# An encoder layer on one core: the norm's weights applied per chunk of 512 tokens, and dummy transposes on TensorE

## The chip, the cores and the metric

The kernel runs on one core of a Trainium2 chip. The metric is the device time of one execution in microseconds; less is better. Before the change it is 1535.71 us, the median of three runs (1535.27 to 1535.77).

## What is computed

One layer of an encoder on 1024 tokens and 16 meta tokens, with 1024 features, in float32:

```python
h = jnp.concatenate([meta_tokens, x], axis=1)          # 16 + 1024 rows
a = rms_norm(h, norm_mix[l])                           # y = x * rsqrt(mean(x*x) + EPS) * g
(q_na, k_na, v_na, q_hg, z_f, z_b, i_hg, g_hg, gate_na, gate_hg) = split_cols(a @ w_in[l])
...
k_f, lf_f = gates(z_fwd, lb[0])                        # lb: a softmax over two rows of logits
k_b, lf_b = gates(z_bwd, lb[1])
...
h = h + mix @ w_o[l]
m = rms_norm(h, norm_mlp[l])
h = h + jnp.square(jax.nn.relu(m @ w_up[l])) @ w_down[l]
h = rms_norm(h, norm_final)
return h[:, N_META:]
```

The change touches only the first lines of this: the norm of the input, its transposition, and the first two products with `w_in`, for the gates `z_f` and `z_b` of the first of four recurrent heads.

## The kernel before

The tokens are cut into two halves (h = 0, 1) of 512. The normed input is held transposed, features on partitions, in `aT[h]`: two tiles of [128, 8, 512], a high part rounded to float32r (`aT_87` and `aT_89` in the lists below) and a low part, the remainder (`aT_88`, `aT_90`). The 16 meta tokens are columns 512 to 527 of half 0. The weights of a column block are split in the same way into `hi` and `lo`, and a product takes three matmuls for each of the eight chunks k of 128 features (`mm3`: L122 hi by high, L123 hi by low, L124 lo by high).

`start()` works on nine tiles of rows: x0 to x7 of 128 tokens and the meta rows `xm`. Each goes through four steps: ScalarE squares it and sums (L554); GpSimd makes the reciprocal root (L92, L93); VectorE multiplies the rows by it and by the norm's weights, which had been spread over all partitions by two products with a row of ones (L542, L545), in one instruction (L559); TensorE transposes eight blocks into two PSUM banks (L567), which ScalarE and VectorE evict as high and low part (L575, L576). Between the tiles stand steps of the first products: `first_products(d, h, ...)` makes gate direction d (0 forward, `z_f`; 1 backward, `z_b`) for a half. `start()` runs the first 256 tokens of direction 0 and half 0 of direction 1; `rest()` runs the others, the last of them direction 1, half 1. Then the projections of `hgrn` follow.

In this stretch the order on each engine is the order in which the code is written (`manual_schedule`). An engine works off its list strictly in order and waits on semaphores. PSUM has eight banks, handed out by tag: "mm" has two, "mx" two, "a" four, each tag in rotation. A new tile in a bank waits until the last reader of the tile that held it before is done, wherever that reader stands in the code:

```python
    banks = {"mm": ctx.enter_context(tc.tile_pool(name="ps_mm", bufs=2, space=PSUM))}
    psum_pools(mx=2, a=4)
```

After the products of one piece, `gates_of` evicts it with two sigmoids on ScalarE (L220, L221) and three instructions on VectorE (L222, L225). The loads of x and of the weight blocks are issued by SP, the small ones by ScalarE's queue.

Of the kernel before, what the change touches and what calls it, by code (L numbers as in the profile page):

```python
# [13 lines left out]
ALU = mybir.AluOpType  # L14
# [34 lines left out]
def layer(ctx: ExitStack, tc: tile.TileContext, x, meta, w_in, w_na, w_hg, w_o, w_up, w_dn,  # L49
# [154 lines left out]
    def gates_of(hd, hp, tiles, done=()):  # L204
# [30 lines left out]
        if hd == 0:  # L235
            yield
            for n_ in range(5):
                d, ps, t0, n, nm = done[n_]
                ev, mev = gate(d)
                if nm:  # L240
                    mev(ps[:, n:])
                ev(ps[:, :n], t0, n)
                yield
            return
# [255 lines left out]
    def first_products(d, h, c0, n, t0, nm):  # L500

        ps = mm_tile(n + nm)
        firsts.append((d, ps, t0, n, nm))
        hi, lo = blocks[d]
        for k in range(KC):
            mm3(ps, hi[:, k], lo[:, k], *(q[:, k, c0:c0 + n + nm] for q in aT[h]), k == 0, k == KC - 1)
            yield

    def start():
        p0s = ExitStack()  # L510
        p0 = p0s.enter_context(tc.tile_pool(name="p0", bufs=1, side="right", reuse_waits="tile"))
        g_bc = p0.tile([P, D], F32, name="g_bc")
        xm = p0.tile([NM, D], F32, name="xm")
        xt = [p0.tile([P, D], F32, tag="xt", name="xt", bufs=8) for _ in range(8)] + [xm]
        lt = p0.tile([P, 2, 2, NHG], F32, name="lt")
        mx = p0.tile([P, 2, NHG], F32, name="mx")
        g_row = p0.tile([1, D], F32, name="g_row")
        ones = p0.tile([1, P], F32, name="ones")
        na, rs = {}, {}
# [4 lines left out]
        def raw_of(col):  # L524
            return load_raw(w_in[:, col:col + P], KC)
        pool.memset(ones, 1.0)
        act.dma_start(g_row, g_mix.rearrange("(o d) -> o d", o=1))
        act.dma_start(xm, meta)
        act.dma_start(lt.rearrange("p a b c -> p (a b c)"), lbl)
        act.dma_start(gain_sb, gain)  # L530
        load_x(0)
        load_x(1)
        raw_f = raw_of(C_ZF)
        for i in range(2, 5):
            load_x(i)
        raw_b = raw_of(C_ZB)
        for i in range(5, 8):
            load_x(i)

        pgs = [bank("a", "pg").rearrange("p a b -> p (a b)") for h in range(2)]  # L540
        for h in range(2):
            pe.matmul(pgs[h], ones, g_row[:, h * TH:(h + 1) * TH], start=True, stop=True)  # L542

        def spread(h):
            act.copy(g_bc[:, h * TH:(h + 1) * TH], pgs[h])  # L545

        def rows(i):
            return NM if i == 8 else P

        def square(i):  # L550
            n = rows(i)
            ssq, rs[i], tm = (p0.tile([P, 1], F32, tag=t, name=t, bufs=6) for t in ("ssq", "rs", "rtm"))
            na[i] = p0.tile([P, D], F32, tag="na", name="na", bufs=4)
            act.activation(na[i][:n], xt[i][:n], AF.Square, accum_out=ssq[:n])  # L554
            rsqrt_mean(rs[i][:n], ssq[:n], D, tm[:n])

        def scale(i):
            n = rows(i)
            dve.scalar_tensor_tensor(na[i][:n], xt[i][:n], rs[i][:n], g_bc[:n], op0=ALU.mult, op1=ALU.mult)  # L559

        def transpose(i):
            n = rows(i)
            pts = []
            for j in range(2):
                pts.append(bank("a", "pt"))
                for k in range(4):
                    pe.transpose(pts[j][:, k, :n], na[i][:n, (4 * j + k) * P:(4 * j + k + 1) * P], ident[:n, :n])  # L567
            return pts

        def evict(i, pts):  # L570
            n = rows(i)
            c0, t = (TH, aT[0]) if i == 8 else (i % 4 * P, aT[i // 4])
            for j in range(2):
                hi, lo = (q[:, 4 * j:4 * j + 4, c0:c0 + n] for q in t)
                act.copy(hi, pts[j][:, :, :n])  # L575
                dve.tensor_tensor(lo, pts[j][:, :, :n], hi.bitcast(F32), op=ALU.subtract)  # L576
# [5 lines left out]
        pts = {}  # L582

        def turn(i):
            pts[i] = transpose(i)

        spread(0)
        square(0)
        spread(1)
        square(1)  # L590
        scale(0)
        turn(0)
        square(2)
        scale(1)
        evict(0, pts[0])
        turn(1)
        blocks[0] = load_block(None, KC, raw=raw_f)
        square(3)
        scale(2)
        evict(1, pts[1])  # L600
        turn(2)
        square(4)
        scale(3)
        evict(2, pts[2])
        f0 = first_products(0, 0, 0, 256, 0, 0)
        some(f0, 4)
        turn(3)
        square(5)
        scale(4)
        evict(3, pts[3])  # L610
        some(f0, 4)
        turn(4)
        square(6)
        blocks[1] = load_block(None, KC, raw=raw_b)
        scale(5)
        evict(4, pts[4])
        b0 = first_products(1, 0, 0, TH, 0, 0)
        some(b0, 2)
        turn(5)
        square(7)  # L620
        scale(6)
        evict(5, pts[5])
        some(b0, 2)
        turn(6)
        square(8)
        scale(7)
        evict(6, pts[6])
        some(b0, 2)
        turn(7)
        scale(8)  # L630
        dve.tensor_tensor(mx, lt[:, :, 0], lt[:, :, 1], op=ALU.max)
# [13 lines left out]
    def rest(gates):  # L645
# [3 lines left out]
        for d, q in ((0, (0, 1, 0, TH, TH, 0)), (0, (0, 0, 256, 256, 256, NM)), (1, (1, 1, 0, TH, TH, 0))):  # L649
            if d:  # L650
                early[C_Q] = block_of(C_Q)
# [975 lines left out]
```

## Time and profile before

| what | value |
|---|---|
| three timed runs | 1535.27 to 1535.77 us, median 1535.71 |
| the profiled execution, span from first to last instruction | 1534.6 us |
| TensorE busy | 1503.2 us, 98% of the span |
| VectorE, ScalarE, GpSimd busy | 67%, 43%, 25% |
| mean busy share of the DMA engines in the first 18 us | near 100% from 3 us on |

The profiled execution is another one than the timed ones, and its own time is known as its span. A busy share is an average over all stages. What a stage costs is read from the order of events in it: which instruction waited, and whose end released it.

### The profile page before, as it was taken

The numbers are of one execution on the slowest core, as the hardware profiler recorded it, in microseconds if no ns is written. First come the engines' busy times: TensorE is split into PE (matmuls) and PEld (weight loads), VectorE is DVE, ScalarE is ACT, GpSimd is POOL, SyncE is SP. The second block draws the span as 40 slices with busy tenths as digits, with TensorE's granted clock in tenths as the row PEclk, the third lists the DMA queues.
The fourth block names the chain that finished last, engine by engine and source line by source line (L and its number), as shares of the span: only waits on it lengthen the run. The fifth ranks groups of instructions, "written<-read, shape, count | busy, mean of one in ns | idle before, by whom it ended". The sixth has DMA issues, their size and how long they took to land.

```text
span 1534.6 us, 23451 instructions
## 1 busy us (share of the span) xinstructions
PE 1503.2 (98%) x9192; PEld 1252.2 (82%) x9192; DVE 1031.3 (67%) x1603; ACT 658.9 (43%) x1175; POOL 380.1 (25%) x354
## 2 busy tenths in 40 slices
PE   7999999999999998999999999999999999999998
PEld 5888888878888887888888887888888888888886
DVE  6676666654876877666476358877777544877876
ACT  6231313125665666434123135555555533434444
POOL 2323131316315400011000122533333300231142
PEclk9999999999999999999999999999999999999999
DMA  4111111114123128434746123444444676563224
GB/s 167 45 29 56 29 56 29 56 29 130 56 66 120 62 65 272 138 124 153 261 163 233 42 97 117 165 154 153 153 153 150 208 266 236 193 232 111 96 83 151
DMA packets 142449, 195.61 MB, mean 127 GB/s; under 512 B 8049, under 2 KB 90097, under 8 KB 142338
## 3 DMA queue, kind: packets, MB, share of 16 engines
q1 hardware_dynamic: 133216, 172.53, 33.9%
q10 hardware_dynamic: 6946, 14.24, 2.4%
q0 software_dynamic: 2176, 7.34, 1.3%
q8 instruction: 72, 1.18, 0.3%
q14 instruction: 39, 0.32, 0.1%
HBM read 139.56 MB, written 54.53 MB: 126 GB/s over the span
## 4 chain that ended last, share of the span: by engine, by line
PE 89%; DVE 5%; issue 2%; ACT 2%; DMA 1%; POOL 1%; ACTq 0%; POOLq 0%; SPq 0%; DVEq 0%
PE mm L122 11%; PE mm L123 11%; PE mm L124 11%; PE mm L1349 5%; PE pa L1349 4%; PE pb L856 4%; PE pb L858 4%; PE pb L857 4%; PE pc L1349 4%; PE pb L1349 4%; PE pc L858 3%; PE pc L857 3%; PE pc L856 3%; PE pa L858 2%; PE pa L857 2%
## 5 line engine op out<-in xcount | busy, mean ns | idle before, releaser
L122 PE MATMUL mm<-aT,hi 128*128 128x512 f32 (+2 forms) x640 | 229.8, 359 | 2.4 <-DVE QX L727 1.5
L124 PE MATMUL mm<-aT,lo 128*128 128x512 f32 (+2 forms) x640 | 226.9, 354 | 0.5 <-DVE lo L113 0.5
L123 PE MATMUL mm<-aT,hi 128*128 128x512 f32 (+2 forms) x640 | 225.8, 353 | 0.0
L122 PEld LDWEIGHTS mm<-aT,hi 128*128 128x128 f32 x640 | 121.4, 190 | 16.6 <-issue 1.7
L124 PEld LDWEIGHTS mm<-aT,lo 128*128 128x128 f32 x640 | 121.3, 190 | 14.2 <-DVE lo L113 1.0
L123 PEld LDWEIGHTS mm<-aT,hi 128*128 128x128 f32 x640 | 121.4, 190 | 12.5
L97 DVE TENSOR_TENSOR dl<-ur,dh 128x1024 fp32r<-128x1024 f32 x54 | 71.0, 1315 | 87.3 <-ACT dh L96 87.1
L96 ACT CAST dh<-ur 128x1024 fp32r<-128x1024 f32 x54 | 56.9, 1054 | 166.5 <-issue 91.1
L112 ACT CAST hi<-raw 128x1024 fp32r<-128x1024 f32 x36 | 37.8, 1050 | 96.7 <-PE mm L123 68.4
L1154 DVE TENSOR_TENSOR wl<-raw,wh 128x512 fp32r<-128x512 f32 x50 | 40.9, 822 | 36.5 <-ACT wh L1153 36.3
L1158 ACT ACTIVATE uv<-uv 128x512 f32<-128x512 f32 x48 | 30.4, 633 | 80.0 <-DVE uv L1266 48.9
L1154 DVE TENSOR_TENSOR wl<-sx,wh 128x512 fp32r<-128x512 f32 x70 | 61.0, 882 | 3.4 <-ACT wh L1153 3.3
L1153 ACT CAST wh<-sx 128x512 fp32r<-128x512 f32 x70 | 42.3, 620 | 42.3 <-PE pc L857 24.0
L1439 POOL TENSOR_TENSOR w<-w,tt 128x512 f32<-128x512 f32 x16 | 23.4, 1460 | 132.9 <-DVE tt L1438 113.2
L300 POOL TENSOR_TENSOR Y<-X,TN 128x512 f32<-128x512 f32 x20 | 34.3, 1713 | 84.5 <-DVE X L297 84.5
L113 DVE TENSOR_TENSOR lo<-raw,hi 128x1024 fp32r<-128x1024 f32 x36 | 46.8, 1300 | 9.8 <-ACT hi L112 9.7
L782 DVE CUSTOM_DVE_ANT_0 pr<-nsc,NB 128x432 f32<-128x432 f32 (+1 forms) x64 | 35.2, 560 | 26.7 <-PE nsc L777 26.5
L409 DVE TENSOR_TENSOR QQ<-QQ,TN 128x512 f32<-128x512 f32 x48 | 35.1, 742 | 22.9 <-PE sc L404 22.9
L856 PE MATMUL pb<-nt,wh 128*128 128x512 f32 x128 | 50.2, 392 | 0.3 <-DVE uv L1236 0.2
L122 PE MATMUL mm<-wh,mT 128*128 128x512 f32 x128 | 50.1, 392 | 0.0
L858 PE MATMUL pb<-nt,wl 128*128 128x512 f32 x128 | 49.8, 389 | 0.0
L124 PE MATMUL mm<-wh,mT 128*128 128x512 f32 x128 | 49.8, 389 | 0.0
(391 smaller groups left out, 4370.9 us busy)
## 6 DMA issues: line engine op xcount, KB each, us to landing
raw<-in_w_in SPq DMA_DIRECT2D x56, 512.0 KB, 4.0
ur<-usp SPq DMA_DIRECT2D x54, 512.0 KB, 3.4
raw<-in_w_up SPq DMA_DIRECT2D x16, 1024.0 KB, 6.1
usp<-us SPq DMA_DIRECT2D x60, 256.0 KB, 2.2
sg<-gsp SPq DMA_DIRECT2D x16, 512.0 KB, 3.3
w<-in_w_dn SPq DMA_DIRECT2D x16, 512.0 KB, 4.5
usp<-uv SPq DMA_DIRECT2D x30, 256.0 KB, 3.2
gsp<-gv ACTq DMA_DIRECT2D x24, 256.0 KB, 2.4
```

What stands on the lines that cost most here:

```text
L96: act.copy(hi, src)
L97: dve.tensor_tensor(lo, src, hi.bitcast(F32), op=ALU.subtract)
L113: dve.tensor_tensor(lo[:, :kc], raw[:, :kc], hi[:, :kc].bitcast(F32), op=ALU.subtract)
L122: pe.matmul(ps, lh, rh, start=first, stop=False)
L123: pe.matmul(ps, lh, rl, start=False, stop=False)
L124: pe.matmul(ps, ll, rh, start=False, stop=last)
L856: pe.matmul(ps, lhs[0][:, c], rhs[0][:, k], start=first and k == 0, stop=False, skip_group_check=True)
L857: pe.matmul(ps, lhs[0][:, c], rhs[1][:, k], start=False, stop=False, skip_group_check=True)
L858: pe.matmul(ps, lhs[1][:, c], rhs[0][:, k], start=False, stop=k == 3, skip_group_check=True)
L1153: act.copy(v(hi), src)
L1154: dve.tensor_tensor(v(lo), src, v(hi).bitcast(F32), op=ALU.subtract)
L1349: pe.matmul(ps, a[n == 2][:, q, j * P:(j + 1) * P], b[n == 1][:, q], start=first and n == 0, stop=last and n == 2, skip_group_check=True)
```

## The change

In the lists and in the code after the change, `warm` is a PSUM tile that nothing reads, `ptm` holds the transposed meta rows, `am` their product with the weights, f0, b0, f1 are the pieces of `first_products` (0, 0), (1, 0) and (0, 1).

- The rows are scaled by their reciprocal root alone, in place (`scale`). The weights come as a column `g_col` of [128, 8] (the host hands in the array in that shape) and are applied at the eviction, to 512 tokens of one chunk of features at a time (`evict(h, k)`): ScalarE writes the high part as a product with the column, VectorE the low part in one instruction. The spreading products and copies are gone.
- A bank now holds one chunk of features of four row tiles (`pts[h, k]`). In the first half six banks are filled side by side, chunks 6 and 7 follow between the first product steps.
- The meta rows come first; they are scaled and transposed into `ptm` in the second bank of tag "mm", and evicted late, behind the scaling of the second half.
- The split of the first two weight blocks is shared out: high part of block 0 on ScalarE, of block 1 on GpSimd, low parts in halves of 512 columns, one of four on VectorE and three on GpSimd.
- The row tile x7 is squared on VectorE. The softmax of `lbl` moves behind the first half's evictions. Half 0 is taken in one product of 512 columns, the 16 meta columns as a piece of their own. The first gate is evicted within `start()`.
- `keep_warm(n)` issues n transposes of the identity into `warm`: 26, then 10, 6, 6 and 5 between the real ones.
- The order of loads becomes x0 to x3, both weight blocks, x4 to x7.

```diff
-    def first_products(d, h, c0, n, t0, nm):
-        ps = mm_tile(n + nm)
-        firsts.append((d, ps, t0, n, nm))
+    def first_products(d, h, tag, n=TH):
+        nm = NM if n == NM else 0
+        c0 = TH if nm else 0
+        ps = bank(tag, "mm").rearrange("p a b -> p (a b)")[:, :n]
+        firsts.append((d, ps, h * TH, n - nm, nm))
...
         def scale(i):
-            n = rows(i)
-            dve.scalar_tensor_tensor(na[i][:n], xt[i][:n], rs[i][:n], g_bc[:n], op0=ALU.mult, op1=ALU.mult)
+            n = xt[i].shape[0]
+            tm = p0.tile([P, 1], F32, tag="rtm", name="rtm", bufs=9)
+            rsqrt_mean(rs[i][:n], sums[i][:n], D, tm[:n])
+            dve.tensor_scalar(xt[i], xt[i], rs[i][:n], None, op0=ALU.mult)
...
+        warm = bank("mm", "warm")
+        def keep_warm(n):
+            for j in range(n):
+                pe.transpose(warm[:, j % 4], ident, ident)
+        def turn(i, ks):
+            for k in ks:
+                pe.transpose(pts[i // 4, k][:, i % 4], xt[i][:, k * P:(k + 1) * P], ident)
+        def chunk(h, k):
+            pts[h, k] = bank("a", "pt")
+            for i in range(4 * h, 4 * h + 4):
+                turn(i, (k,))
+        def evict(h, k):
+            hi, lo = (t[:, k, :TH] for t in aT[h])
+            pt = pts[h, k].rearrange("p a b -> p (a b)")
+            act.mul(hi, pt, g_col[:, k:k + 1])
+            dve.scalar_tensor_tensor(lo, pt, g_col[:, k:k + 1], hi.bitcast(F32), op0=ALU.mult, op1=ALU.subtract)
...
+        keep_warm(26)
+        square(8)
+        scale(8)
+        ptm = bank("mm", "ptm")[:, 0].rearrange("p (k t) -> p k t", t=NM)
+        for k in range(KC):
+            pe.transpose(ptm[:, k], xt[8][:, k * P:(k + 1) * P], ident[:NM, :NM])
+        keep_warm(10)
+        for k in range(6):
+            pts[0, k] = bank("a" if k < 4 else "mx", "pt")
+        for i in range(4):
+            square(i)
+            scale(i)
+            turn(i, range(6))
+            if i < 3:
+                keep_warm(6 - i // 2)
+        block(0)
+        block(1)
+        low(0, dve, A)
+        low(0, pool, B)
+        low(1, pool, A)
+        low(1, pool, B)
+        f0 = first_products(0, 0, "mm")
+        evict(0, 0)
+        evict(0, 1)
+        for k in range(6):
+            some(f0, 1)
+            if k < 2:
+                chunk(0, k + 6)
+            evict(0, k + 2)
...
+        some(f0, 2)
+        for i in (4, 5, 6):
+            square(i)
+            if i == 4:
+                act.activation(lts, lts, AF.Exp)
+                pool.tensor_tensor(mx, lt[:, :, 0], lt[:, :, 1], op=ALU.add)
         scale(4)
+        square(7, dve)
+        for i in (5, 6, 7):
+            scale(i)
         dve.reciprocal(mx, mx)
...
+        b0 = first_products(1, 0, "mm")
+        some(b0, 6)
+        dve.tensor_tensor(am, ptm, fap(g_col, 0, [[1, KC], [0, NM]]), op=ALU.mult)
+        act.copy(mh, am)
+        dve.tensor_tensor(ml, am, mh.bitcast(F32), op=ALU.subtract)
+        f1 = first_products(0, 1, "mx")
+        for k in range(KC):
+            chunk(1, k)
+            evict(1, k)
+            if k == 0:
+                next(gates)
+            if k < 2:
+                some(b0, 1)
+            if k > 2:
+                some(f1, 1)
```

What stands on an engine's list shows where the change puts things. First the start of TensorE's list, before the change (`na` are the scaled rows, `pg` the spread weights; in brackets the engines whose semaphores the row waits for, Activation is ScalarE, Pool is GpSimd):

```order
L542 MATMUL pg<-g_row,ones 128x512 [waits DMAHW0_49,Pool_49]
L542 MATMUL pg<-g_row,ones 128x512
L567 MATMUL pt<-ident,na 128x128 [waits DVE_49]
L567 MATMUL pt<-ident,na 128x128 x7
L567 MATMUL pt<-ident,na 128x128 [waits DVE_49]
```

And after it:

```order
L557 MATMUL warm<-ident 128x128 [waits Pool_49]
L557 MATMUL warm<-ident 128x128 x25
L594 MATMUL ptm<-ident,xm 128x16 [waits DVE_49]
L594 MATMUL ptm<-ident,xm 128x16 x7
L557 MATMUL warm<-ident 128x128 x10
L561 MATMUL pt<-ident,xt 128x128 [waits DVE_49]
L561 MATMUL pt<-ident,xt 128x128 x5
L557 MATMUL warm<-ident 128x128 x6
```

The two spreading products are gone; 26 dummies, the meta transposes and ten more dummies stand ahead of the first rows of x, and six more behind them.

Next TensorE's list after the change where f0 ends and b0 begins (the last row of step 6 of f0, steps 7 and 8 cut short, and the first rows of b0):

```order
L124 MATMUL mm<-aT_87,lo 128x512
L122 MATMUL mm<-aT_87,hi 128x512 [waits Activation_49]
L123 MATMUL mm<-aT_88,hi 128x512 [waits DVE_49]
...
L124 MATMUL mm<-aT_87,lo 128x512
L122 MATMUL mm<-aT_87,hi 128x512 [waits DVE_49]
L123 MATMUL mm<-aT_88,hi 128x512
L124 MATMUL mm<-aT_87,lo 128x512 [waits Pool_49]
L122 MATMUL mm<-aT_87,hi 128x512
```

In f0 a first product (L122) waits for ScalarE, which wrote its operand `aT_87`. The first product of b0 reads the same `aT_87` and a `hi` that GpSimd wrote, and waits for VectorE.

Last VectorE's list after the change, from the end of the first half's evictions to the first of the second half:

```order
L572 SCALAR_TENSOR_TENSOR aT_88<-pt,g_col,aT_87 128x512 [waits Activation_49] x2
L551 TENSOR_SCALAR xt<-xt,rs 128x1024 [waits DMAHW2_49,Activation_49,Pool_49]
L544 ISA junk,ssq<-xt 128x1024 [waits DMAHW5_49,Activation_49]
L544 ISA ssq 128x1
L551 TENSOR_SCALAR xt<-xt,rs 128x1024 [waits DMAHW3_49,Pool_49]
L551 TENSOR_SCALAR xt<-xt,rs 128x1024 [waits DMAHW4_49,Activation_49,Pool_49]
L551 TENSOR_SCALAR xt<-xt,rs 128x1024 [waits DVE_49,Pool_49]
L632 RECIPROCAL mx<-mx 128x8
L637 TENSOR_TENSOR am<-ptm,g_col 128x128
L639 TENSOR_TENSOR aT_88<-am,aT_87 128x8x16 [waits Activation_49]
L572 SCALAR_TENSOR_TENSOR aT_90<-pt,g_col,aT_89 128x512 [waits Activation_49]
```

The only reader of `ptm` stands behind all four scalings of the second half. From the first product of the query block (`C_Q`) on, the lists of all engines hold the same computing work in the same order in both kernels.

## Rows read from the trace of the kernel before

**Rows 1.** The page: the span, and the chain that ended last by engine.

```profile
span 1534.6 us, 23451 instructions
...
PE 89%; DVE 5%; issue 2%; ACT 2%; DMA 1%; POOL 1%; ACTq 0%; POOLq 0%; SPq 0%; DVEq 0%
```

**Rows 2.** TensorE's waits, whole span: us in total, times, longest us.

```profile
PE pt L567 <- DVE na L559: 4.4, 2, 2.3
...
PE ppt L797 <- DVE PT L809: 2.6, 1, 2.6
```

**Rows 3.** Timeline of TensorE, 3 to 49 us: start, us, what, count.

```profile
3.31 3.75 PE L542 MATMUL pg<-g_row,ones 1*128 1x512 f32 x4 [3.31 <-DMA g_row<-in_g_mix]
9.33 3.97 PE L567 MATMUL pt<-ident,na 128*128 128x128 f32 x16 [2.27 <-DVE na L559]
15.46 1.94 PE L567 MATMUL pt<-ident,na 128*128 128x128 f32 x8 [2.17 <-DVE na L559]
...
19.76 1.91 PE L567 MATMUL pt<-ident,na 128*128 128x128 f32 x8
...
22.95 1.04 PE L567 MATMUL pt<-ident,na 128*128 128x128 f32 x8
...
29.27 1.07 PE L567 MATMUL pt<-ident,na 128*128 128x128 f32 x8
...
31.66 1.06 PE L567 MATMUL pt<-ident,na 128*128 128x128 f32 x8
...
48.25 0.39 PE L123 MATMUL mm<-aT,hi 128*128 128x512 f32 x1
48.47 0.39 PE L124 MATMUL mm<-aT,lo 128*128 128x512 f32 x1
```

**Rows 4.** Timeline, all engines, first 100 us: two of the issues of loads.

```profile
1.28 0.35 ACTq L528 DMA_DIRECT2D xm<-in_meta  x1
...
2.10 3.07 SPq L522 DMA_DIRECT2D xt<-in_x  x3
```

**Rows 5.** DMA view, issues at 1.28 and 2.10 us: KB each, us to landing.

```profile
xm<-in_meta ACTq DMA_DIRECT2D x1, 64.0 KB, 4.7
...
xt<-in_x SPq DMA_DIRECT2D x1, 512.0 KB, 7.2
```

**Rows 6.** Timeline of ScalarE: a square, two evictions, a table load.

```profile
5.87 1.06 ACT L554 ACTIVATE na<-xt 128x1024 f32<-128x1024 f32 x1
...
27.54 1.07 ACT L575 CAST aT<-pt 128x512 fp32r<-128x512 f32 x2 [1.24 <-PE pt L567]
...
34.99 1.28 ACT L220 ACT_TABLE_LOAD   x1
```

**Rows 7.** Timeline of VectorE: a scaling, two evictions, a tensor_scalar of 512 columns.

```profile
7.99 1.28 DVE L559 SCALAR_TENSOR_TENSOR na<-xt,rs,g_bc 128x1024 f32<-128x1024 f32 x1 [7.99 <-POOL rs L93]
...
15.23 1.28 DVE L576 TENSOR_TENSOR aT<-pt,aT 128x512 fp32r<-128x512 f32 x2
...
37.50 0.55 DVE L222 TENSOR_SCALAR T<-sf,oml_sb,lb_sb 128x512 f32<-128x512 f32 x1
```

**Rows 8.** Groups by form on GpSimd, whole span: busy us, mean ns, idle before.

```profile
L187 POOL TENSOR_TENSOR rt<-aT,aT 128x512 f32<-128x512 f32 x16 | 22.5, 1405 | 12.7 <-DMA tsp_t<-rt 12.2
...
L699 POOL MEMSET KL<- 64x1152 f32 x1 | 1.1, 1057 | 0.1
```

**Rows 9.** Stretches: length, busy of PE, PEld, DVE, ACT, POOL, clock, DMA, GB/s.

```profile
18.00:21.00 3.00, 3.00 (x16) 3.00 (x15) 2.10 (x3) 1.22 (x4) 1.54 (x2) 1.00 0.01 2
```

**Rows 10.** Timeline of TensorE in the attention stage: products of 128 columns.

```profile
395.50 0.22 PE L820 MATMUL pov<-PT,Vn 128*128 128x128 f32 x1
395.55 0.22 PE L821 MATMUL pov<-PT,Vn 128*64 128x128 f32 x1
```

**Rows 11.** Timeline of TensorE, its last product.

```profile
1527.16 0.39 PE L1349 MATMUL pa<-dh,dl 128*128 128x512 f32 x1
```

**Rows 12.** Stretches, the last one (columns as in rows 9).

```profile
1530.00:1534.60 4.60, 0.00 (x0) 0.00 (x0) 0.75 (x1) 0.72 (x1) 0.00 (x0) 0.53 0.59 228
```

More of the change, by code (lines that the diff above doesn't have):

```diff
@@ L538, in start @@
+        for i in range(4, 8):
             load_x(i)
[L540 to L550, printed above, removed]
-            n = rows(i)
[L552 to L555, printed above, removed]
@@ L557, in scale, with square @@
-        def scale(i):
-            n = rows(i)
-            dve.scalar_tensor_tensor(na[i][:n], xt[i][:n], rs[i][:n], g_bc[:n], op0=ALU.mult, op1=ALU.mult)
[L561 to L576, printed above, removed]
+        def square(i, eng=act):
+            t = xt[i]
+            n = t.shape[0]
+            sums[i], rs[i] = (p0.tile([P, 1], F32, tag=q, name=q, bufs=9) for q in ("ssq", "rs"))
+            junk = p0.tile([P, D], F32, tag="junk", name="junk", bufs=2)
+            if eng is act:
+                act.activation(junk[:n], t, AF.Square, accum_out=sums[i][:n])
+            else:
+                dve.tensor_tensor_reduce(out=junk[:n], in0=t, in1=t, scale=1.0, scalar=0.0,
+                                         op0=ALU.mult, op1=ALU.add, accum_out=sums[i][:n])
@@ L580, in some @@
                 next(steps)
[L582 to L605, printed above, removed]
@@ L628, in start, with block @@
[L628 to L631, printed above, removed]
-        pool.tensor_tensor(lt[:, :, 0], lt[:, :, 0], mx, op=ALU.subtract)
-        pool.tensor_tensor(lt[:, :, 1], lt[:, :, 1], mx, op=ALU.subtract)
-        some(b0, 2)
-        evict(7, pts[7])
-        turn(8)
-        act.activation(lt.rearrange("p a b c -> p (a b c)"), lt.rearrange("p a b c -> p (a b c)"), AF.Exp)
-        evict(8, pts[8])
-        pool.tensor_tensor(mx, lt[:, :, 0], lt[:, :, 1], op=ALU.add)
+        def block(d):
+            blocks[d] = [wp.tile([P, KC, P], F32R, tag=t, name=t) for t in ("hi", "lo")]
+            (pool.tensor_copy if d else act.copy)(blocks[d][0], raws[d])
@@ new lines, in low @@
+        def low(d, eng, c):
+            hi, lo = blocks[d]
+            eng.tensor_tensor(lo[:, c], raws[d][:, c], hi[:, c].bitcast(F32), op=ALU.subtract)
+        A, B = slice(0, 4), slice(4, 8)
+        lts = lt.rearrange("p a b c -> p (a b c)")
+        mh, ml = (t[:, :, TH:TH + NM] for t in aT[0])
+        keep_warm(26)
[4 more added lines that the diff above has]
+            pe.transpose(ptm[:, k], xt[8][:, k * P:(k + 1) * P], ident[:NM, :NM])
@@ L668, in layer @@
         tiles = [[] for _ in range(NHG + 1)]
-        ahead = [gates_of(hd, hp, tiles[hd], firsts if hd == 0 else ()) for hd in range(NHG)] + [iter(())]
+        ahead = [gates_of(hd, hq, tiles[hd], firsts if hd == 0 else ()) for hd in range(NHG)] + [iter(())]
         next(ahead[0])
-        rest(ahead[0])
+        f1 = start(ahead[0])
+        hp = hps.enter_context(tc.tile_pool(name="hp", bufs=1, reuse_waits="tile"))
+        rest(ahead[0], f1)
         psum_pools(mx=1, a=3, b=2)
```

78 lines of the change are left out of this document (27 added, 51 removed).

## The prediction

> **What bounds the kernel now.** I read the page first: of a span of 1534.6 us the chain that ended last spends 89% in TensorE [rows 1]. Then TensorE's waits over the whole span: the largest group is the transposes of the input norm waiting for VectorE's scaled rows, 4.4 us in two waits; a wait later on is 2.6 us at most [rows 2]. The change touches only the start, so I looked for a mark at which both kernels are in the same place: the last product of the fourth piece, direction 1 and half 1. Before, it starts at 48.47 us, and at a pitch of 0.22 to 0.23 us the piece is over at 48.7 [rows 3]. Behind the mark the four engines' lists have the same computing work in the same order, and TensorE almost never waits there, so I let a shift of the mark pass to the end one to one. The timed median, 1535.71 us, lies 1.1 us above the profiled span; I add the shift to the median. A measurement of this kernel can tell about 0.2%, or 3.1 us, from no change.
>
> TensorE's own rows before the mark show two rates. Eight transposes take 1.91 us at 19.76 and 1.04 us at 22.95 [rows 3]: 0.24 and 0.12 us each (0.13 with the tail), so 1.2 GHz until about 21.3 us and 2.4 GHz from there. (The column of the granted clock reads 1.00 from the start, the durations don't.) What went ahead of the rise was work without a pause from 15.46 us on, 5.9 us of transposes and products mixed.
>
> **The front up to the first products.** Nothing of the weights' row is needed any more: two products on one partition and two ScalarE copies go. The first transfer on ScalarE's queue is now the meta rows: issued 0.56 us sooner than the 1.28 us of before and landed after the same 4.7 us [rows 4, 5], that is at 5.4. ScalarE's five squares (meta, x0 to x3) follow each other at 1.06 us [rows 6]: they begin at 5.4, 6.5, 7.5, 8.6 and 9.6. x3 takes the place in the queue that x2 had, issued at 2.10 and landed 7.2 us on, at 9.3 [rows 4, 5], so it isn't late. From the start of a square to the start of its scaling went 2.12 us (5.87 to 7.99) [rows 6, 7]. The scaling loses its second operand; no row has it at 1024 columns. It lies between 0.55 us (a tensor_scalar of 512 columns) and 1.28 us (the old form) [rows 7]; I take 0.85. So scaled meta rows are there at 8.4 and x3 at 12.6.
>
> TensorE gets there later. After the eight short meta transposes (0.6 us) 51 transposes stand in its list, 24 real and 27 dummies; at 0.12 us that is 6.1 us, so the last ends at 15.1, 2.5 us after x3 is scaled at 12.6. This holds if the 26 first dummies, from about 1.5 us on without a pause, have brought 2.4 GHz by then.
>
> The first half's evictions cost ScalarE 0.54 us and VectorE 0.64 us a chunk [rows 6, 7] against three products of 0.23 us, so TensorE sets the pace: low part of chunk 0 at 15.8 (eviction behind the first finished bank, 14.5 + 0.55 + 0.65 + 0.1), then eight steps of 0.69 and two groups of four transposes of 0.5, to 22.1 us. GpSimd's share, a cast of 1024 columns and three subtractions of 512, costs 1.06 us (a memset of 1152 columns) to 2.8 us (two tensor_tensors) for the cast and 1.4 us for each of the others [rows 8]. I take 1.6 for the cast, as it has one input only: from about 12 to 18 us. ScalarE's Exp waits for what follows it, but not before 19.6, so the upper value costs nothing either.
>
> **A wait that the change adds.** Tag "mm" has two banks. In the order of allocation they go to warm, ptm, f0 and b0: b0's bank is the one that holds the transposed meta rows. They are read by one VectorE instruction, am, which stands behind the scalings of x4 to x7 and the reciprocal. The order shows a wait for VectorE on b0's very first product, whose operands come from ScalarE and GpSimd, and whose f0 counterpart had waited for ScalarE alone. So b0's six steps, which stand ahead of the transposes of the second half, can't fill the gap that these leave. Behind them on TensorE's queue stands everything else.
>
> When does am end? ScalarE's last eviction needs chunk 7 (about 18.0) and ends at 18.6. Squares of x4, x5, x6 start at 18.6, 19.9 (behind Exp) and 20.9; the rows are in SBUF by then, as the transfers are over at 18 [rows 9]. VectorE: scaling x4 20.8 to 21.7 (2.12 us after its square, and a small GpSimd step), square of x7 to 23.0 (1.3 us; bounds 1.1, an element a cycle as the squares on ScalarE have it, and 2.6, twice the old scaling), x5 and x6 to 24.7, x7 to 25.55, reciprocal and am 0.4: 26.0. TensorE pauses from 22.1 to 26.0, 3.9 us. With the bounds am ends between 25.0 and 28.0.
>
> **From there to the mark.** 18 products of b0, 4.1 us. The old pattern of eight transposes and six products took 2.39 us (29.27 to 31.66) [rows 3]; half of each is 1.2 us, seven such pairs are 8.4. One group of transposes alone 0.5, three steps 2.1, a wait of 0.2 for the second chunk of half 1, whose eviction stands behind a table load of 1.28 us and two sigmoids on ScalarE [rows 6]; but for b0's late steps this would be a long wait. Sum 15.3, at 41.3. The first half is no longer cut at 256 columns, and meta's 24 products have 16 columns. Products of 128 columns with a full weight load followed each other at 0.055 us [rows 10]; I take 0.06: 1.5 us, at 42.8. The fourth piece 5.5: the mark at **48.3, 0.4 us sooner** than before, at the full clock.
>
> **The clock in the new pause.** After the last product of the kernel, ending at 1527.55, the stretch 1530 to 1534.6 has a mean granted clock of 0.53 [rows 11, 12], so it fell to half (1.2 GHz) at about 1530.3, 2.7 us into silence; the pause of 2.6 us in rows 2 didn't lower it. A pause of 3.9 us is beyond both. What a fall costs: the one rise in the trace came after 5.9 us of work at the low rate [rows 3], which loses half of it, 2.9 us; the least is nothing, if the fall comes and goes within the pause. I take three quarters, 2.2 us, since part of the time at 1.2 GHz will lie in the pause itself. The sum is -0.4 + 2.2 = **+1.8 us, 1537.5 us**.
>
> **Rivals.** *The pause doesn't lower the clock* (or am ends sooner, at 25): -0.4 us, 1535.3. For it speaks that 2.6 us were too short; against it, that 2.7 at the end were not.
>
> *Dummy transposes don't bring the full clock.* Then the 51 transposes cost 0.24 us each, 12.2 us instead of 6.1, the evictions and the chain behind them to am start 6.1 us later, and some of f0 runs at the low rate: 1535.3 + 6.1 + 0.5 is about 1542, slower by 0.4%. It decides from the point where the meta transposes still run at 1.2 GHz. The trace leaves it open: ahead of the one rise there were both products and transposes. For "they count" speaks that 3.75 us of products on one partition at 3.31 us brought nothing [rows 3], so products alone weren't enough there either. The Trainium skill, "TensorE: Matmul & The Clock Gate", Part 4: PE-mode transpose, says that transposes don't engage the full clock, because they don't count as busy in the same way; by that rule this rival would be the forecast, and no row here decides.
>
> *The shared bank costs nothing*, because am is done when f0 ends: b0's steps fill the pause, 3.9 us less than the full-clock sum, 1531.4, faster by 0.3%. It needs the chain of squares and scalings four us sooner; with each us that it is sooner, one us is won. Against it stand six 1024-column passes on VectorE behind 18.6 us.
>
> **How the numbers follow.** Forecast 0.45, no fall of the clock 0.2, dummies that don't count 0.25, cheap bank 0.1. The range, 1533.6 to 1542.2, holds the first two with the bounds of am (-1.0 and +2.0 us) and the clock (0 to 2.9), and half of the third; the likeliest case alone spans 1535.5 to 1540. Faster by over 0.2%: 0.1, the last rival. Slower: the third rival and the upper end of the first, 0.33. Within: 0.57.
>
> **What would show it.** In the changed profile: eight transposes at 0.12 us each from some 8 us on (right) or at 0.24 until 20 us; a wait of TensorE for am of about 4 us, at 22 us, the largest of the kernel; first products of b0 at a pitch of 0.43 us if the clock fell; 24 products of 16 columns in 1.5 us; the mark at 50.5 us. The forecast is wrong if the wait is short, if turned x3 is late for another reason (a transfer), or if what lies behind the mark doesn't keep its length.

## The result, and the profile after the change

The changed kernel takes 1540.93 us, the median of five runs (1539.44 to 1543.14). The kernel before, in the same set of runs, takes 1535.53 us (1533.73 to 1535.77). The ratio is 1.0038, with an interval of 1.0026 to 1.0051: slower by 5.4 us, where 1.8 us were forecast. The time lies inside the predicted range, 3.4 us above the predicted value. The profiled execution took 1543.14 us over a span of 1541.4 us.

First the page of the changed kernel, its head and the chain that ended last; these lines answer to [rows 1]:

```profile
span 1541.4 us, 23535 instructions
...
PE 88%; DVE 5%; issue 2%; ACT 2%; DMA 2%; POOL 1%; ACTq 0%; POOLq 0%; DVEq 0%
```

The shares of the chain differ from those of before by one per cent at most (TensorE 88 for 89, DMA 2 for 1), so the page alone doesn't show where the time went. TensorE's waits over the whole span do (us in total, times, longest us); compare [rows 2]:

```profile
PE mm L122 <- DVE am L637: 5.3, 1, 5.3
PE sc L405 <- DVE QQ L410: 2.6, 4, 0.8
PE ppt L806 <- DVE PT L818: 2.3, 1, 2.3
```

The two waits of 4.4 us for scaled rows are gone from the top. In their place stands one wait of 5.3 us, now the longest of the kernel, for `am`: the VectorE instruction that reads the transposed meta rows. TensorE's timeline of the start answers to [rows 3]:

```profile
1.35 4.46 PE L557 MATMUL warm<-ident 128*128 128x128 f32 x26 [1.35 <-POOL ident masks.py:199]
...
8.69 0.82 PE L561 MATMUL pt<-ident,xt 128*128 128x128 f32 x6
...
13.67 0.87 PE L561 MATMUL pt<-ident,xt 128*128 128x128 f32 x6 [0.87 <-DVE xt L551]
...
22.05 0.39 PE L124 MATMUL mm<-aT,lo 128*128 128x512 f32 x1
27.72 0.80 PE L122 MATMUL mm<-aT,hi 128*128 128x512 f32 x1 [5.28 <-DVE am L637]
28.32 0.63 PE L123 MATMUL mm<-aT,hi 128*128 128x512 f32 x1
28.74 0.63 PE L124 MATMUL mm<-aT,lo 128*128 128x512 f32 x1
...
33.74 0.60 PE L561 MATMUL pt<-ident,xt 128*128 128x128 f32 x4
...
44.95 0.17 PE L122 MATMUL mm<-aT,hi 128*128 128x16 f32 x1
...
47.55 0.49 PE L122 MATMUL mm<-aT,hi 128*128 128x512 f32 x1
...
48.92 0.63 PE L124 MATMUL mm<-aT,lo 128*128 128x512 f32 x1
...
54.70 0.39 PE L122 MATMUL mm<-aT,hi 128*128 128x512 f32 x1
```

The mark (the fourth piece is over and the next one starts) is at 54.70 us, 6.0 us behind the 48.70 of before. Products of 512 columns follow each other at 0.43 us from 28.32 on, at 0.23 later, and again at 0.43 from 48.92. The view by stretches shows why (length; busy time of PE, PEld, DVE, ACT and POOL; granted clock; DMA share; GB/s):

```profile
4.40:24.70 20.30, 15.07 (x104) 12.47 (x102) 14.24 (x19) 14.31 (x26) 15.77 (x23) 1.00 0.79 271
24.90:31.50 6.60, 3.78 (x9) 3.01 (x10) 2.07 (x5) 0.30 (x1) 1.91 (x5) 0.50 0.00 0
...
45.00:47.50 2.50, 2.50 (x25) 2.50 (x23) 1.24 (x3) 1.09 (x2) 1.21 (x1) 1.00 0.03 7
...
48.80:52.00 3.20, 3.20 (x9) 2.42 (x9) 1.22 (x1) 0.12 (x1) 1.99 (x6) 0.50 0.18 48
```

The granted clock falls to half (1.2 GHz) twice: in the pause, and at 48.7 us, where TensorE has been busy without a gap, with the 24 products of 16 columns before it (45.00 to 47.50 is busy for the whole 2.50 us).

Why `am` is late is seen on VectorE, whose timeline answers to [rows 7], and on GpSimd, which makes the reciprocal roots. First VectorE:

```profile
23.71 0.75 DVE L551 TENSOR_SCALAR xt<-xt,rs 128x1024 f32<-128x1024 f32 x1 [0.44 <-POOL rs L93]
25.18 0.75 DVE L551 TENSOR_SCALAR xt<-xt,rs 128x1024 f32<-128x1024 f32 x1 [0.71 <-POOL rs L93]
26.65 0.75 DVE L551 TENSOR_SCALAR xt<-xt,rs 128x1024 f32<-128x1024 f32 x1 [0.71 <-POOL rs L93]
27.32 0.20 DVE L632 RECIPROCAL mx<-mx 128x8 f32<-128x8 f32 x1
27.43 0.24 DVE L637 TENSOR_TENSOR am<-ptm,g_col 128x128 f32<-128x128 f32 x1
```

Then GpSimd in the same stretch:

```profile
20.52 0.19 POOL L92 TENSOR_SCALAR rtm<-ssq 128x1 f32<-128x1 f32 x1
...
25.23 0.75 POOL L92 TENSOR_SCALAR rtm<-ssq 128x1 f32<-128x1 f32 x1
26.07 0.55 POOL L93 TENSOR_TENSOR rs<-rtm,half 128x1 f32<-128x1 f32 x1
```

A scaling takes 0.75 us, but one starts only every 1.47 us. GpSimd's first small operation takes 0.19 us while VectorE doesn't scale (20.52) and 0.75 us when it begins beside a scaling (25.23, behind the scaling of 25.18): it ends with the scaling, then the root follows (0.55), and only then the next scaling. The two engines take turns; e5 below tests this.

### The profile page after: what moved, and what is told of

It reads as the page before. It is cut to its first block, busy times and chain, and to the rows that moved or that the text cites. A ratio compares the mean times of both kernels' runs of the same rounds, so it can differ in the third digit from the quotient of the medians.

```text
span 1541.4 us, 23535 instructions
## 1 busy us (share of the span) xinstructions
PE 1508.4 (98%) x9241; PEld 1258.5 (82%) x9241; DVE 1030.7 (67%) x1601; ACT 657.4 (43%) x1167; POOL 386.0 (25%) x357
## 4 chain that ended last, share of the span: by engine, by line
PE 88%; DVE 5%; issue 2%; ACT 2%; DMA 2%; POOL 1%; ACTq 0%; POOLq 0%; DVEq 0%
PE mm L122 11%; PE mm L123 11%; PE mm L124 11%; PE mm L1358 5%; PE pa L1358 4%; PE pb L865 4%; PE pb L866 4%; PE pb L867 4%; PE pc L1358 4%; PE pb L1358 4%; PE pc L865 3%; PE pc L867 3%; PE pc L866 3%; PE pa L866 2%; PE pa L867 2%
## 5 line engine op out<-in xcount | busy, mean ns | idle before, releaser
L122 PE MATMUL mm<-aT,hi 128*128 128x512 f32 (+2 forms) x640 | 231.8, 362 | 8.2 <-DVE am L637 5.3
L122 PEld LDWEIGHTS mm<-aT,hi 128*128 128x128 f32 x640 | 121.8, 190 | 23.6 <-DVE am L637 5.7
L122 PE MATMUL mm<-wh,mT 128*128 128x512 f32 x128 | 50.2, 392 | 0.0
L123 PE MATMUL mm<-wl,mT 128*128 128x512 f32 x128 | 49.9, 390 | 0.0
```

The lines of the kernel that those rows point to most:

```text
L122: pe.matmul(ps, lh, rh, start=first, stop=False)
L123: pe.matmul(ps, lh, rl, start=False, stop=False)
```

## The theories, and the experiments

**Theory.** The loss is made ahead of the mark: b0's bank is the one that `am` has to free, TensorE stands still, the clock falls, and the 16-column piece adds its own time. **Rivals.** The dummies cost or bring the time; the clock is what costs, not the wait; or the time is lost behind the mark.

Each kernel below is compared with runs of the kernel before on the same chip. The marks are read from each kernel's one profiled execution: the first product of 256 columns behind the mark starts 10.88 us after it in both kernels, and the marks are that row's start less 10.88 (in e3, which waits in between, the mark is read directly). The changed kernel itself came out at 1.0038 in one set of runs and at 1.0057 in another (e9), so ratios from different sets can be compared to some 0.2% only.

| kernel | mark, us | median, us | ratio to before | interval |
|---|---|---|---|---|
| before, two profiles | 48.70, 47.74 | 1534.98 to 1535.53 | | |
| changed kernel | 54.70 | 1540.93 | 1.0038 | 1.0026 to 1.0051 |
| e1 own bank | 46.92 | 1536.38 | 1.0009 | 1.0000 to 1.0018 |
| e2 pause filled | 51.64 | 1540.37 | 1.0037 | 1.0025 to 1.0050 |
| e3 meta mixed | 53.70 | 1544.68 | 1.0064 | 1.0050 to 1.0078 |
| e4 no dummies | 54.37 | 1542.04 | 1.0051 | 1.0039 to 1.0064 |
| e5 roots batched | 52.71 | 1542.96 | 1.0048 | 1.0034 to 1.0062 |
| e6 before + dummies | 46.27 | 1534.90 | 0.9998 | 0.9989 to 1.0007 |
| e7 meta early | 44.44 | 1534.03 | 0.9992 | 0.9983 to 1.0001 |
| e8 e7 + e5 | 46.71 | 1536.10 | 1.0005 | 0.9997 to 1.0014 |
| e9 changed, again | 55.11 | 1544.60 | 1.0057 | 1.0044 to 1.0070 |
| e11 e7, split earlier | 44.45 | 1533.01 | 0.9984 | 0.9976 to 0.9993 |
| e12 e11, no dummies | 45.47 | 1531.61 | 0.9977 | 0.9966 to 0.9987 |

**e1, a bank of its own for b0.** One word:

```diff
-        b0 = first_products(1, 0, "mm")
+        b0 = first_products(1, 0, "mx")
```

> The changed kernel with one word changed: b0 takes a bank of tag mx instead of the one that holds the transposed meta rows. Theory: that shared bank makes TensorE wait 5.3 us for am, and the pause lowers the clock; without it six steps of b0 run between 22.4 and 26.5 us, a pause of about 1 us is left until x7 is scaled at 27.4, no fall of the clock near 25 us, and the end of the fourth piece moves from 54.7 to 47 to 48.5 us: 6 to 8 us off the changed kernel's time, 1533 to 1535 us. Rival (the time goes to the evictions of the second half, whose place b0 only hides): b0's steps move ahead, but TensorE then waits as long for the second half's chunks, and less than 2 us is won.

The wait for `am` is gone, and the clock stays up from 5.3 us to the mark. TensorE's longest group of waits up to 50 us, and the stretch:

```profile
PE pt L561 <- DVE xt L551: 1.4, 2, 0.8
...
5.30:46.90 41.60, 37.93 (x228) 31.60 (x227) 26.84 (x44) 24.73 (x45) 21.45 (x35) 1.00 0.41 141
```

The mark comes 7.8 us sooner than in the changed kernel. Of this, 1.65 us are the changed kernel's fall of the clock at 48.7 us, which e9 will show to belong to that execution. The shared bank and the pause that hangs on it are the other 6.1 us, about the whole loss at the mark. The median falls by 4.55 us only; the last paragraph of this section comes back to that.

**e2, the pause filled.** The wait stays, and 44 more dummies stand in it:

```diff
+        warm = bank("mx", "warm2")
+        keep_warm(44)
         b0 = first_products(1, 0, "mm")
```

> The changed kernel with 44 more dummy transposes (4.7 us at 0.107) on TensorE's list between f0 and b0, into a bank of tag mx; the wait for am stays. It separates the pause from the fall of the clock that follows it. Theory: b0's first product still starts at about 27.7 us, but at a pitch of 0.23 instead of 0.43 us, and the fourth piece ends 1.9 us sooner (1539.0 us). Rival (transposes don't keep the clock up, as they only raised it here after a start from rest): the clock falls in spite of them, and the time is the changed kernel's within 0.5 us. The fall after the products of 16 columns is untouched in both.

```profile
22.57 4.97 PE L557 MATMUL warm<-ident 128*128 128x128 f32 x44
28.02 0.50 PE L122 MATMUL mm<-aT,hi 128*128 128x512 f32 x1 [0.47 <-DVE am L639]
```

These rows of TensorE's timeline show the dummies at 0.11 us each and b0 behind them at the full rate. So the clock stayed up in the same pause once TensorE was kept at work in it, and dummy transposes were enough for that. The mark is 3.1 us sooner than in the changed kernel: 1.8 us of b0's products (4.2 us for 18 instead of 6.0) and the 1.65 of the second fall, which isn't there either, less 0.3 by which b0 begins later. The medians, 1540.37 and 1540.93, can't be told apart: with the wait kept, keeping the clock up won nothing that can be measured.

**e3, the 16-column products spread over the fourth piece:**

```diff
-        list(first_products(0, 0, "mm", NM))
+        m16, b1 = first_products(0, 0, "mm", NM), first_products(1, 1, "mx")
+        for k in range(KC):
+            next(m16)
+            next(b1)
...
-        list(first_products(1, 1, "mx"))
+        list(b1)
```

> The changed kernel with the 24 products of 16 columns no longer in one block but three at a time between the steps of the fourth piece (same work, other order; the meta gate's eviction comes later). Theory: the block of 16-column products, 2.6 us long, lowers the clock at about 48.7 us although TensorE is never idle, and costs 1.7 us in the fourth piece; mixed with products of 512 columns it doesn't, so the stretch from the first 16-column product to the end of the fourth piece takes 7.0 to 8.1 us instead of 9.75, and the time falls by 1.7 to 2.8 us. Rival (the second fall is a late consequence of the pause at 22 us, and comes whatever runs at 48 us): the stretch keeps its 9.75 us within 0.5.

```profile
53.70 0.49 PE L122 MATMUL mm<-aT,hi 128*128 128x512 f32 x1 [0.48 <-ACT hi L112]
...
54.96 0.51 PE L124 MATMUL mm<-aT,lo 128*128 128x512 f32 x1 [0.53 <-DVE lo L113]
```

A miss: from the first 16-column product (44.81) to the mark it takes 8.9 us, against 2.6 + 5.6 in e1, of which 0.5 us is the first of the two waits in these rows. Spreading didn't make the small products cheaper, and as the meta rows' gate came later, so did the cast of the next weights, for which TensorE waits here and once more just behind the mark.

**e4, no dummies:**

```diff
-        keep_warm(26)
...
-        keep_warm(10)
...
-            if i < 3:
-                keep_warm(6 - i // 2)
```

> The changed kernel without its 53 dummy transposes, wait for am and all else kept. Theory: TensorE stays at 1.2 GHz until some 4 to 6 us into f0 (before the change the rise came after 5.9 us of work), f0 ends 1 to 3 us later, everything behind it too; 1542 to 1544 us. Rival (the front hangs on the loads and the scaling of x3 at 13.6 us, and TensorE makes up for it in the pause of 5.3 us, so the dummies buy nothing here): within 0.5 us of the changed kernel.

```profile
7.27 1.03 PE L587 MATMUL ptm<-ident,xm 16*128 16x16 f32 x8 [7.27 <-DVE xm L551]
8.76 4.48 PE L555 MATMUL pt<-ident,xt 128*128 128x128 f32 x18 [0.46 <-DVE xt L551]
13.92 0.88 PE L555 MATMUL pt<-ident,xt 128*128 128x128 f32 x6 [0.68 <-DVE xt L551]
```

TensorE's timeline: 18 real transposes at 0.24 us still wait for x3 at 13.92 us, where the changed kernel had been at 13.67. The clock rose by 13.6 us without any dummy. The dummies take TensorE's time, not the path's: f0's last product starts at 22.30 us without them, at 22.05 with them. The mark is as late as in the changed kernel though the second fall is missing, because the fall in the pause lasted longer here (27.2 to 34.0 us; b0's 18 products took 7.0 us).

**e5, the roots in batches** (x0 with x1, x2 with x3, x4 to x7):

```diff
-        scale(4)
         square(7, dve)
-        for i in (5, 6, 7):
-            scale(i)
+        scale(4, 5, 6, 7)
```

> The changed kernel with one edit: the reciprocal roots of the rows are taken on GpSimd for x0 and x1 together, for x2 and x3, and for x4 to x7, and the scalings on VectorE follow in one go (the square of x7 goes ahead of them). In the changed kernel the scalings start 1.47 us apart though one lasts 0.75, and GpSimd's small operation beside each is stretched from 0.19 to 0.75 us. Theory (GpSimd is kept out while VectorE scales, so the two alternate): scalings of one group 0.7 us apart; x3 scaled near 12.4 instead of 13.6 us; the transposed meta rows read near 25.2 instead of 27.4; pause of TensorE 4 us instead of 5.3; mark 2 to 2.2 us sooner (52.5 if the clock falls in the pause, near 50.6 if not); time 1538.7 (or 1537). Rival (a scaling simply takes its turn every 1.47 us, whoever makes the root): still 1.47 us apart, mark near 54.7, time near 1540.5.

GpSimd's two rows for the roots of x4 to x7, and VectorE's scalings:

```profile
22.01 0.20 POOL L92 TENSOR_SCALAR rtm<-ssq 128x4 f32<-128x4 f32 x1 [2.18 <-DVE ssq L543]
22.29 1.01 POOL L93 TENSOR_TENSOR rs<-rtm,half 128x4 f32<-128x4 f32 x1
...
23.33 2.74 DVE L556 TENSOR_SCALAR xt<-xt,rs 128x1024 f32<-128x1024 f32 x4 [1.49 <-POOL rs L93]
```

TensorE's first product of b0:

```profile
26.39 0.80 PE L122 MATMUL mm<-aT,hi 128*128 128x512 f32 x1 [4.61 <-DVE am L642]
```

Four scalings in 2.74 us instead of one each 1.47 us: the taking of turns is shown. `am` starts 1.3 us sooner (26.10), and so does b0 (26.39 against 27.72). The mark comes 2.0 us sooner, near the 52.5 expected, but not by these 1.3 us alone: the fall in the pause cost 1.0 us more (b0's 18 products took 7.0 us), and the second fall of 1.65 us didn't come. The time doesn't follow; its interval overlaps the changed kernel's, and the two were run in different sets.

**e6, the dummies alone, in the kernel before:**

```diff
+        keep_warm(26)
         spread(0)
...
         turn(0)
+        keep_warm(10)
...
         turn(1)
+        keep_warm(10)
```

> The kernel before with one edit: 26 dummy transposes at the start and 10 each behind the transposes of the first and of the second 128 rows. Theory (dummies bring the full clock): the clock is at full rate by 5 us, transposes and products at 15 to 21 us go at 0.12 us instead of 0.21 to 0.24; at most 2.9 us won at the mark (48.7 before); as evictions and scalings pace the front in part, 1 to 2.5 us, mark 46 to 47.7, time 1533 to 1534.5. Rival (dummies don't count as work for the clock): rise near 21 us as before, mark and time as before.

```profile
6.21 4.43 PE L591 MATMUL warm<-ident 128*128 128x128 f32 x26
10.48 1.04 PE L567 MATMUL pt<-ident,na 128*128 128x128 f32 x8
```

Eight transposes at 10.48 us take 1.04 us, where before it was 3.97 for sixteen [rows 3]. The dummies ran behind the spreading products, not ahead of them, and the clock rose at 9.1 us, not by 5 as expected. The mark comes 1.5 to 2.4 us sooner, and the median stays where it was (0.9998).

**e7, the meta rows read early, and no piece of 16 columns:**

```diff
+            if i == 0:
+                dve.tensor_tensor(am, ptm, ...)
+        act.copy(mh, am)
...
-        f0 = first_products(0, 0, "mm")
+        f0 = first_products(0, 0, "mm", 0, 256)
+        f0m = first_products(0, 0, "mm", 256, 256, NM)
...
-        b0 = first_products(1, 0, "mm")
+        b0 = first_products(1, 0, "mx")
...
-        list(first_products(0, 0, "mm", NM))
```

> The changed kernel with three places edited: the transposed meta rows are read and split early (behind the scaling of x0), first products of direction 1 have the other tag's bank, and the half 0 of direction 0 is cut into 256 and 256+16 columns as before, so that no piece of 16 columns is left. Theory: no wait of 5 us at 22 us, no clock fall there and none at 48 us, since both stand behind what is taken away; f0 ends within 0.5 us of 22.3; the mark near 44.7 (own bank alone had 46.9; the 24 products of 16 columns took 2.6 us and 16 more columns elsewhere cost 0.3), 4 us sooner than before the change. Time 1531.5 if the shift arrives whole, 1534 if as much gets lost behind the mark as with the own bank alone. Rival (the 16 columns' 2.6 us were hidden or are paid in the wider products): mark near 47, time 1536.

The mark is where the theory puts it, 44.44 us, 10.3 us ahead of the changed kernel: 7.8 us as in e1 (with the second fall that is missing in both), and 2.5 us more because the 16 columns now ride on another piece. VectorE's timeline shows what is left to gain:

```profile
12.77 1.53 DVE L583 TENSOR_TENSOR lo<-raw,hi 128x512 fp32r<-128x512 f32 x1
14.22 1.35 DVE L609 TENSOR_TENSOR aT<-am,aT 128x128 fp32r<-128x128 f32 x1
15.49 0.74 DVE L571 SCALAR_TENSOR_TENSOR aT<-pt,g_col,aT 128x512 fp32r<-128x512 f32 x1
```

A subtraction of 128 columns takes 1.35 us (0.29 in the changed kernel), as GpSimd works on its own subtractions beside it, and the first eviction waits behind it.

**e8, e7 with the batches of e5.**

> The kernel e7_meta_early with the batched roots of e5_roots_batched. Theory: f0 starts 1 us sooner and the transposes of half 1 no longer wait for scaled rows (1.4 us in two waits with the own bank alone); mark 1 to 2.5 us sooner than e7_meta_early, near 43; time 1530 to 1533, below the kernel before by 0.15 to 0.35%. Rival (the front hangs on something else, a load or GpSimd's halves of the weights): mark as in e7_meta_early.

```profile
11.60 2.28 DVE L555 TENSOR_SCALAR xt<-xt,rs 128x1024 f32<-128x1024 f32 x2 [1.51 <-POOL rs L93]
...
17.90:21.10 3.20, 3.20 (x17) 3.20 (x16) 3.20 (x7) 0.69 (x1) 0.23 (x3) 0.50 0.81 233
```

A miss: the mark is 2.3 us later than in e7. The second group of scalings (x2 and x3) took 2.28 us instead of 1.42, as GpSimd's cast of the weights began at 12.30 beside it, and in this execution the clock was at half for 3.2 us of f0, as the stretch shows. Such a fall can cost some 1.7 us (the one at 48.7 us in the changed kernel cost 1.65), so the mark alone doesn't tell how much the batches did. The median is 2.1 us above e7's in the same set, so they didn't help.

**e9 and e10, the changed kernel and the kernel before once more,** for a second profile of each.

> The changed kernel itself once more, for a second profile. In its first profile the clock fell twice, in the pause at 25 us and behind the 24 products of 16 columns at 48.6 us; in four experiments with the same 24 products it did not fall behind them. Theory A (the small products lower the clock in every execution of this kernel): two falls again, mark 54 to 55. Theory B (the second fall is a matter of the execution): one fall, mark 52.8 to 53.2, and the median of this kernel stands for a mark between the two. Time 1540 to 1541.5 in both.

> The kernel before once more, for a second profile. Theory A (the clock rises near 21 us in every execution): mark 48.5 to 49. Theory B (the rise is anywhere between 12 and 21 us by execution): mark between 46.3, which it has with dummies that bring the full clock, and 48.7. By B the gains at the mark that the experiments show against 48.7 are too large by up to 2.4 us, which would account for what their medians lack.

Three stretches of e9, and two rows of TensorE's timeline in e10:

```profile
590.40:593.60 3.20, 3.20 (x10) 2.56 (x9) 3.20 (x7) 3.12 (x8) 0.00 (x0) 0.50 0.62 195
17.00:20.00 3.00, 3.00 (x13) 2.61 (x12) 3.00 (x6) 1.55 (x3) 1.26 (x3) 0.50 0.83 232
27.20:33.80 6.60, 4.38 (x10) 3.48 (x11) 1.74 (x5) 0.30 (x1) 1.39 (x4) 0.50 0.00 0
```

```profile
19.35 1.32 PE L567 MATMUL pt<-ident,na 128*128 128x128 f32 x8
...
58.62 0.28 PE L122 MATMUL mm<-aT,hi 128*128 128x256 f32 x1
```

In e9 the clock doesn't fall behind the 16-column products, so theory A falls; it falls in f0 instead, and the mark is as late as in the first profile. The fall in the pause is there both times, and in e3, e4 and e5, but of different cost: b0's 18 products took 5.6 us (e3), 6.0, 6.3 (e9) and 7.0 (e4, e5) instead of 4.1; the stretch at 590 us shows one far behind the mark. On this third chip the changed kernel takes 1544.60 us, 3.7 us more than in the first set, with before at 1535.48: the loss is 5.4 to 9.1 us, with 6.0 to 7.4 at the mark. In e10 the clock rises 1.6 us sooner (at 19.9), and the mark is 1.0 us sooner (58.62 less 10.88).

**e11, e7 with the split of the meta rows ahead of x3's scaling:**

```diff
+            if i == 2:
+                act.copy(mh, am)
+                dve.tensor_tensor(ml, am, mh.bitcast(F32), op=ALU.subtract)
```

> e7_meta_early with the split of the meta rows moved ahead of x3's scaling on VectorE, where it no longer stands before the first eviction's low part (there it took 1.35 us, and the second product waited 1.9 us). Theory: VectorE's first eviction 1.2 us sooner, f0's wait 0.7 us instead of 1.9, f0 ends 22.0 and the mark 1.0 to 1.3 us ahead of e7_meta_early; time 1533, 0.15% below the kernel before. Rival (x3's scaling moves back by as much as the split takes): mark as in e7_meta_early.

```profile
16.29 0.39 PE L123 MATMUL mm<-aT,hi 128*128 128x256 f32 x1 [0.84 <-DVE aT L571]
```

The wait of f0's second product fell as expected, from 1.9 to 0.84 us, but the rival holds: x3 came 1.0 us later (transposed at 13.96, in e7 at 12.92), the second product starts at 16.29 us in both, and the mark is e7's. The median is 2.5 us below before.

**e12, e11 without dummies:**

```diff
-        keep_warm(26)
...
-        keep_warm(10)
...
-                keep_warm(6 - i // 2)
```

> e11_meta_early2 without any dummy transpose. Theory (the front hangs on the scaling of x3 and on the evictions, and the real transposes bring the clock up by themselves): clock up by 14 us, mark within 0.7 us of e11_meta_early2, time as there within 1 us. Rival (the dummies carry it): f0 at the low rate, mark 2 to 4 us later.

```profile
15.00:19.90 4.90, 4.01 (x20) 3.81 (x21) 4.90 (x9) 3.57 (x6) 3.16 (x5) 0.69 0.71 234
```

Part of f0 ran at the low rate here (0.69 on the mean), and the mark is 1.0 us later than with dummies. That isn't a late rise: the clock was up at 13.5 us and fell from 16.9 to 20.3, as it did in f0 of e8 and e9 with all their dummies. The time isn't: 1531.61 us is the lowest median of all, 3.9 us below before, 0.9977 (0.9966 to 0.9987). Its interval overlaps e11's, so this says that the dummies buy nothing that can be measured, not that they cost something. Both versions have the mark and the median below those of both kernels, e12 by 0.23% (0.13 to 0.34%), e11 by 0.16% (0.07 to 0.24%).

**What the experiments leave open.** Shifts of the mark don't reach the median whole. In the profiled executions the rest of the span, from the mark to its end, is 1485.5 and 1485.9 us for before, 1486.7 and 1487.5 for the changed kernel, and 1485.3 (e12) to 1488.3 us (e8) for the others apart from e3 (1489.2). Some executions have another fall of the clock near 580 to 615 us (e1, e3, e4, e7 and e9; neither profile of before), but the rest isn't longer with it throughout: e4 has it and 1485.9. By its mark alone e1 should beat before by 0.8 to 1.8 us; its median is 1.4 us above.

The 8996 products behind the mark are the same, in the same order, in every profile, so their starts can be set against those of before one by one. But for e3 they drift apart in two places only: between 220 and 620 us, by up to 2.4 us, and at one wait near 720 us. Elsewhere the distance keeps within about 0.2 us. A fall at 580 to 590 us costs 1.3 to 1.4 us on the spot (e1, e4, e7, e9), and most of it is gone again by 608 us; the 1.6 us of e3's fall, at 615, stay. Two waits of TensorE make up much of the difference; in order, one of the changed kernel near 490 us that neither profile of before has, one near 720 us in before, and the same one in e8:

```profile
PE mm L122 <- DVE KL L745: 0.6, 1, 0.6
```

```profile
PE pb L856 <- DVE gv L949: 0.2, 1, 0.2
```

```profile
PE pb L872 <- DVE gv L965: 1.5, 1, 1.5
```

The first is there in eight of the eleven profiles of the changed kernel and its variants (not in e4, e5 and e12); the other is 1.5 us in e5 too and 0.9 in e12. So the rest takes up the shift of the mark differently from kernel to kernel. What decides whether these waits come wasn't found.

## Why the prediction was right in direction and too small

**Point by point, up to the pause.** *The dummies bring the full clock*: right. The 26 dummies alone, with no other work ahead of them, raised it at 4.3 us (at 4.1 to 7.0 in the other executions that begin with them), and the six transposes at 8.69 took 0.82 us; the second rival falls. The Trainium skill, "TensorE: Matmul & The Clock Gate", Part 4: PE-mode transpose, says that the full clock doesn't engage for transposes; these traces, with 128x128 transposes in float32, show that it does. *The front*: f0 ends at 22.3 us against 22.1, but not by the steps that were given. The meta rows landed 3.1 us after their issue instead of 4.7, and the squares began behind a table load, at 4.07 us instead of 5.4. The scalings came every 1.47 us instead of every 1.06, and x3's, beside GpSimd's cast of the weights, lasted 1.57, so x3 was done at 13.6 instead of 12.6. The forecast had left 2.5 us between x3 and the end of the transposes (15.1). These took less than assumed and waited for x3, and ended at 14.5. That f0's end came out right is in part luck.

**The wait that the change adds**: right in its place and cause, and the largest of the kernel, as forecast. Its size was 5.3 us against 3.9, because `am` ended at 27.7 instead of 26.0. The term that failed is the four scalings at 0.85 us each, one behind the other. A scaling took 0.75, less than assumed, but the step left out that GpSimd's roots can't run beside it. Of the 1.7 us, 0.6 were there when x4's scaling began (21.4 us instead of 20.8), and 1.1 came from the turns behind it. e5 showed this by taking the roots out of between: 1.3 us. The Trainium skill, "SBUF — State Buffer", section Who interferes with whom, states the rule: VectorE and GpSimd have a pair of ports in common, a VectorE operation of the scaling's kind can hold it for its whole length, and GpSimd then stands still. The trace agrees: 0.75 us beside a scaling, 0.19 without one.

**The clock in the pause**: right. It fell at 24.8 us, 2.3 us into silence (the prediction had a silence of 2.6 us without a fall), and 18 products of b0 took 6.0 us (27.72 to 33.74) instead of 4.1: 1.9 us against the 2.2 taken. The first rival (no fall) falls with it; and so does the third (the bank that costs nothing), since e1, with another bank and nothing else changed, has its mark 7.8 us sooner, 6.1 without the second fall.

**From there to the mark**: the pairs of transposes and products took 11.2 us (33.74 to 44.95), as forecast (15.3 less 4.1). The piece of 16 columns was mis-sized: 2.6 us instead of 1.5, 0.111 us a product. The bound came from a row of products of 128 columns at 0.055 us [rows 10], and I took narrow products to be as cheap. The row was also misread: of its two products only one has weights of 128 columns, the other has 64 (128*64). In the stretch 45.00 to 47.50 the weight loads (PEld) are busy for the whole 2.50 us, 23 of them. That speaks for a price per load and not per column; no run tests it. The fourth piece took 7.15 us instead of 5.5, since the clock fell once more at 48.7. That wasn't foreseen; e1, e2, e4, e5 and e9 have the same products in the same order without that fall, so it belongs to the execution.

The sum: forecast 50.5 us at the mark; +1.7 for `am`, -0.3 for the clock, +1.1 for the small products, +1.65 for the second fall make 54.65, and 54.70 was measured. Of the 4.2 us that the forecast lacked at the mark, 2.5 are terms of the kernel that were too small, and 1.65 are of this execution. That a shift of the mark goes one to one into the median held for the changed kernel in the first set (6.0 and 5.4 us), less well in e9's (6.4 to 7.4 and 9.1), and didn't hold for e1, e2, e5 and e6. The prediction had let it pass because TensorE almost never waits behind the mark; the few waits that there are changed by up to 1.3 us.

## What to carry to other kernels

When a tile's bank is handed on by rotation, look for the last reader of the tile that had it, and for what stands ahead of that reader on its engine: here one small instruction behind four scalings held up TensorE's whole list, and one word undid it. When two engines feed each other, time the pair (1.47 us), not each alone (0.75 and 0.75): batching the small step breaks the alternation, if nothing else of the second engine runs beside it (here it shortened the wait by 1.3 us, and no time that can be measured). And narrow products cost by the piece: append columns to a wider product rather than give them products of their own (2.5 us at the mark in e7).

## What the runs showed of the hardware

Dummy transposes alone brought the clock to its upper level and held it there (26 from 1.35 us on; 44 in a pause of 5 us). The clock isn't the same from execution to execution of one kernel: the changed kernel fell at 24.8 and 48.7 us in one profile, at 16.8 and 27.1 in the other, and several kernels were at half for some 3 us of f0 or near 580 to 615 us while TensorE was busy for most of that time (the stretch of 3.0 us in e9 above was busy throughout). Products of 16 columns followed each other at 0.111 us at the full clock, twice the 0.055 of the two products with 128 columns in [rows 10], of which one had only half the weights. And a VectorE subtraction of 128 columns took 1.35 us beside GpSimd's subtractions (e7), and 0.29 us without them (the changed kernel).
